# The last two tiles' search for 256 keys moves from the latent projections into the latent attention sweep, with its rows in the places of h

## The chip, the cores and the metric

The kernel runs on one core of a Trainium2 chip. The metric is the device time of one execution in microseconds. Five engines matter: TensorE (PE, with its weight loads PEld), VectorE (DVE), ScalarE (ACT), GpSimd (POOL) and SyncE (SP), which issues the DMA transfers here. Each engine runs its own instructions in order.

## The reference

Two layers. Each normalises x (2048 positions, 1024 wide), projects it, and mixes it in four groups of heads, whose gated outputs are joined and projected back.

```python
y_a = stick_breaking(a_q, a_k, a_v)                    # group A, 4 heads of 64
cq, ckv = rms_norm(b_cq, ...), rms_norm(b_ckv, ...)    # group B, latents of 256 and 128
qb, kv = cq @ mla_w_uq, ckv @ mla_w_ukv                # 4 heads, 64 + 32 rotary
y_b = softmax_attention(q, k, v_b, 96 ** -0.5)
# group C: an indexer scores all visible keys of a query and keeps the best 256
score = sum over 4 index heads of iw * relu(iq . ik / 8)
top_val, top_idx = lax.top_k(score, 256)
y_c = softmax over those keys only
# group D: two softmaxes a head, subtracted: w = p1 - lam * p2
y_d = rms_norm(diff_attention(...), ...) * (1 - lam_init)
y = concatenate(silu(gate) * y_group); x = x + y @ w_out
```

All attention is causal by chunks of 64 keys. The queries go in 16 blocks (tiles) of 128, so tile i sees 128 (i + 1) keys.

## The kernel before, in words

**Sweeps.** A layer goes through the 16 tiles seven times, in the order a, h, d0, d1, b, c, o: group A with the indexer's scores (a); the projections of group B's latents and of two gates (h); the two halves of group D (d0, d1); the attention of group B on its latents, the latent sweep (b); the sparse attention (c); the output (o). `drive` (L1391) hands out, with tile t's attention, the load of h for tile t + 4, `prep` of tile t + 2 and `proj` of tile t + 3, across the ends of sweeps too; the weights of a sweep are handed out four and five tiles before it. So b's projection of tile 7 is handed out with b's tile 4.

**Order.** The program is Python that writes instructions; a planner then orders them. It simulates the engines and gives each the earliest instruction, by the order of writing, whose data and buffers are there. `at` (L306) shifts a part's place in that order: the search is written in 30 places ahead, projections and preparations 10 places behind (`LATER`). On the chip the order of each engine is then fixed.

**Buffers.** The pool `wk` has tiles by name with a number of places: `g2` (4), `h_hi` and `h_lo` (2 each, 4096 bytes a partition each), `x4a`, `x4b`, `x4c` (1 each), `hl` (2). Two rings of bytes hold what changes size: `ring` (R1) the weights, keys and values of the sweeps, `rows` (R2) the rows of attention (`rw`), of scores (`sc`) and of the search (`sg`). A row of tile i has 512 (i + 1) bytes a partition: 7680 for tile 14, 8192 for tile 15.

**The search.** `ci_score` (L490) writes a tile's scores to DRAM. `ci_search` (L527) takes a pair of tiles, loads their rows (L535) and looks for a threshold that 256 keys exceed. ScalarE counts with a sign and an accumulator (L549); VectorE turns the count into the next threshold in some 18 small instructions (L551, L612 to L633). There are two counts at fixed points, then eight rounds. Then four long passes a tile on VectorE mark the keys (L641, L643, L644, L651), and the marks go to DRAM (L653), from where sweep c's `prep_c` (L983) takes them. Each `yield` ends a step. `SEARCH` says where a pair's search is written: pairs up to (10, 11) within sweep a, (12, 13) and (14, 15) both with tile 3 of h (`search_at`, called in `proj_h`). The rows of tiles 14 and 15 lie in `ring` (`INBIG`), the others in `rows`, where there is room for tile 13's only when earlier ones are done.

**The projections.** `proj_d` (L1026) copies v out of PSUM (L1033), takes squares on ScalarE, sums on VectorE (L1039), 1/sqrt on GpSimd (`rstd`, L282 and L283), the rotation on VectorE (L1092 to L1095), and GpSimd writes the parts `hl` (L197, L191) that TensorE then transposes. `proj_b` loads a tile's latents into a `g2` (L1241), splits them into two further `g2`, and uses `g2` for the squares (L1253 to L1256), for t, r, u and w too: nine a tile.

Of the kernel before, what the change touches and what calls it, by code (L numbers as in the profile page):

```python
# [10 lines left out]
F32 = mybir.dt.float32  # L11
# [4 lines left out]
AF = mybir.ActivationFunctionType  # L16
OP = mybir.AluOpType
AX = mybir.AxisListType
# [4 lines left out]
D = 1024  # L23
# [3 lines left out]
BIG = 1.0e30  # L27
# [9 lines left out]
EARLY = (10, 11, 9)  # L37
SEARCH = {("a", 4): ((2, 3),), ("a", 7): ((4, 5),), ("a", 10): ((6, 7),), ("a", 15): ((8, 9), (10, 11)), ("h", 3): ((12, 13), (14, 15))}
HL = 2
QA = 3  # L40
EV = (0.6, 1.0, 0.6)
INBIG = (14, 15)
ST = 2
# [12 lines left out]
LATER = {"search": -30, "prep": 10, "proj": 10, "first": 10, "second": 0}  # L56
R1 = 88832
R2 = 30592

# [48 lines left out]
class Trunk:  # L108
    def __init__(self, ctx, tc, I, out, layers=2):
        self.tc, self.nc, self.I, self.out, self.layers = tc, tc.nc, I, out, layers  # L110
        nc = self.nc
        e = ctx.enter_context
# [16 lines left out]
        ct = self.cst.tile  # L129
# [11 lines left out]
        nc.gpsimd.memset(self.nego, -1.0)  # L141
        self.eps = ct([128, 1], F32, name="eps")
        nc.vector.memset(self.eps, EPS)
# [4 lines left out]
        self.junk = ct([128, S], I8, name="junk")  # L148
        self.chkA = ct([128, layers], F32, name="chkA")
        self.chkC = ct([128, layers, NT], F32, name="chkC")  # L150
        nc.vector.memset(self.chkC, float(TOPK))
        self.ev = 0

    def constants(self):
# [371 lines left out]

    def ci_search(self, l, b):  # L527

        nc, wk = self.nc, self.wk
        yield 100.0  # L530
        tl, G = b, len(b)
        ns = [128 * (i + 1) for i in tl]
        Sg = [(self.ring if i in INBIG else self.rows).tile([128, n], F32, name="sg") for i, n in zip(tl, ns)]
        for g in range(G):
            nc.sync.dma_start(Sg[g], self.sc[tl[g]])  # L535
        stt = lambda nm: wk.tile([128, G], F32, name="st_" + nm, bufs=ST)
        V = nc.vector
        tt, ts, sst, cp = V.tensor_tensor, V.tensor_scalar, V.scalar_tensor_tensor, V.copy_predicated
# [7 lines left out]
        def count(dst, th):  # L546

            for g in range(G):
                nc.scalar.activation(self.junk[:, :ns[g]], Sg[g], AF.Sign, bias=th[:, g:g + 1], scale=-1.0,  # L549
                                     accum_out=dst[:, g:g + 1])  # L550
            sst(dst, dst, -0.5, nh, op0=OP.mult, op1=OP.add)  # L551
# [3 lines left out]
        for g in range(G):  # L555
            V.max(m8[:, g, :], Sg[g][:, ::32])
            V.tensor_reduce(a[:, g:g + 1], Sg[g][:, :ns[g] - 64:32], axis=AX.X, op=OP.max, apply_absolute_value=True)
        zt = stt("zt")
# [79 lines left out]
        for g in range(G):  # L638
            i = tl[g]
            ge = wk.tile([128, S], I8, name="ge", bufs=1)[:, :ns[g]]  # L640
            ts(ge, Sg[g], T[:, 0, g:g + 1], 0.0, op0=OP.is_ge, op1=OP.add, accum_out=T[:, 1, g:g + 1])  # L641
            yield 0.0
            sst(Sg[g], ge, -BIG, Sg[g], op0=OP.mult, op1=OP.add)  # L643
            V.max(ex[:, g, 1:9], Sg[g])  # L644
            ts(rc[:, g:g + 1], T[:, 1, g:g + 1], -1.0, float(TOPK), op0=OP.mult, op1=OP.add)
            oh = wk.tile([128, 9], F32, name="st_oh")
            ts(oh, self.iota9, rc[:, g:g + 1], None, op0=OP.is_equal)
            V.tensor_tensor_reduce(oh, oh, ex[:, g, :], 1.0, 0.0, OP.mult, OP.add, sp[:, g:g + 1])
            yield 0.0
            ck = self.chkC[:, l, i:i + 1]  # L650
            sst(ge, Sg[g], sp[:, g:g + 1], ge, op0=OP.is_lt, op1=OP.subtract, accum_out=ck)  # L651
            ts(ck, ck, -1.0, float(ns[g]), op0=OP.mult, op1=OP.add)
            nc.sync.dma_start(self.out_of[i][:, :ns[g]], ge)  # L653
            yield 0.0
# [23 lines left out]
    def search_at(self, l, sweep, i):  # L678
        if not self.short:
            return  # L680
        gs = [self.at(LATER["search"], self.ci_search(l, b)) for b in SEARCH.get((sweep, i), ())]
        while gs:
            for g in list(gs):
                if next(g, None) is None:
                    gs.remove(g)

    def prep_a(self, l, i, st):
# [549 lines left out]
    def proj_b(self, l, i, st):  # L1237
        nc, wk = self.nc, self.wk
        yield 1600.0
        raw = self.g2([128, 3, 128])  # L1240
        nc.sync.dma_start(raw, self.cT[i])  # L1241
# [9 lines left out]
                       kv[:, :, 64:])  # L1251
        sq = self.g2([128, 4, 96])
        nc.scalar.activation(sq[:, :, :64], qv[:, :, :64], AF.Square, scale=0.125)  # L1253
        nc.scalar.activation(sq[:, :, 64:], qv[:, :, 64:], AF.Square, scale=32 ** -0.5)
        sk = self.g2([128, 4, 64])
        nc.scalar.activation(sk, kv[:, :, :64], AF.Square, scale=0.125)  # L1256
# [5 lines left out]
        t = self.g2([128, 8, 64])  # L1262
        r = self.g2([128, 5, 32])
        nc.sync.dma_start(r[:, 4, :], self.kr[i])
# [7 lines left out]
        yield 0.0  # L1272
        u = self.g2([128, 5, 32])
        w = self.g2([128, 5, 32])
        cs = wk.tile([128, 2, 64], F32, name="ci_cs")[:, :, :32]
# [235 lines left out]
```

## Time and profile before

| | us |
|---|---|
| median of 3 runs | 4197.03 |
| lowest and highest | 4191.1, 4197.24 |
| profiled execution, its own time | 4202.9 |
| span of its instructions | 4201.0 |
| TensorE busy | 3887.7 |
| VectorE busy | 2784.5 |
| ScalarE busy | 2321.2 |
| GpSimd busy | 1361.0 |

Times in the rows below count from the start of the span. The mean granted clock of TensorE is 0.951, as a share of full speed. In the first layer the sweeps lie roughly so: a to 450, h to 620, d0 to 980, d1 to 1255, b to 1615, c to 1930, o to 2100; the second layer repeats this.

### The profile page before, as it was taken

The numbers are of one execution on the slowest core, as the hardware profiler recorded it, in microseconds if no ns is written. First come the engines' busy times: TensorE is split into PE (matmuls) and PEld (weight loads), VectorE is DVE, ScalarE is ACT, GpSimd is POOL, SyncE is SP. The second block draws the span as 40 slices with busy tenths as digits, with TensorE's granted clock in tenths as the row PEclk, the third lists the DMA queues.
The fourth block names the chain that finished last, engine by engine and source line by source line (L and its number), as shares of the span: only waits on it lengthen the run. The fifth ranks groups of instructions, "written<-read, shape, count | busy, mean of one in ns | idle before, by whom it ended". The sixth has DMA issues, their size and how long they took to land. (4 is left out here: it accounts for less than half of the span.)

```text
span 4201.0 us, 75220 instructions
## 1 busy us (share of the span) xinstructions
PE 3887.7 (93%) x25833; PEld 3279.2 (78%) x25833; DVE 2784.5 (66%) x10279; ACT 2321.2 (55%) x4799; POOL 1361.0 (32%) x2188
## 2 busy tenths in 40 slices
PE   7998998898978999999999989868989889999998
PEld 7887887777857888778888878767788668877787
DVE  3798677886876655663348975778768666556622
ACT  4566577565655555463246656675656555455621
POOL 2233222454553433310033331224445544232100
PEclk9999997899989999999999999879999799999999
DMA  4323562232210013225422246522222100132144
GB/s 135 104 97 122 176 192 88 76 93 78 86 38 23 18 38 106 77 67 175 166 98 98 94 127 204 161 66 79 87 86 82 36 23 18 39 111 72 59 142 141
DMA packets 227880, 396.49 MB, mean 94 GB/s; under 512 B 66336, under 2 KB 150432, under 8 KB 226976
## 3 DMA queue, kind: packets, MB, share of 16 engines
q1 hardware_dynamic: 227488, 391.59, 29.5%
q8 instruction: 207, 3.39, 0.3%
q14 instruction: 185, 1.52, 0.1%
HBM read 279.00 MB, written 112.49 MB: 93 GB/s over the span
## 5 line engine op out<-in xcount | busy, mean ns | idle before, releaser
L267 PE MATMUL pj<-w_hi,h_hi 128*128 128x384 f32 (+4 forms) x2560 | 875.8, 350 | 48.5 <-ACT w_hi L204 19.0
L268 PE MATMUL pj<-w_lo,h_hi 128*128 128x384 f32 (+4 forms) x2560 | 861.8, 344 | 8.4 <-POOL w_lo L191 6.3
L860 ACT ACTIVATE rw<-rw,at_mn 128x896 f32<-128x896 f32 (+15 forms) x512 | 616.1, 1205 | 191.4 <-DVE at_mn L859 161.0
L294 PE MATMUL tp<-ident,rw 128*128 128x128 f32 x3264 | 535.2, 288 | 55.4 <-DVE rw L1125 31.6
L267 PEld LDWEIGHTS pj<-w_hi,h_hi 128*128 128x128 f32 x2560 | 504.7, 197 | 81.1 <-ACT w_hi L204 21.3
L296 ACT COPY pt<-tp 128x512 f32<-128x512 f32 (+3 forms) x689 | 356.4, 530 | 381.5 <-PE tp L294 356.6
L268 PEld LDWEIGHTS pj<-w_lo,h_hi 128*128 128x128 f32 x2560 | 504.6, 197 | 34.8 <-POOL w_lo L191 9.9
L271 PE MATMUL pj<-w_hi,h_lo 128*128 128x384 f32 (+4 forms) x2560 | 527.5, 337 | 0.6 <-POOL h_lo L191 0.5
L294 PEld LDWEIGHTS tp<-ident,rw 128*128 128x128 f32 x3264 | 381.0, 145 | 167.0 <-issue 69.8
L271 PEld LDWEIGHTS pj<-w_hi,h_lo 128*128 128x128 f32 x2560 | 436.7, 191 | 24.7 <-issue 8.8
L856 DVE TENSOR_SCALAR_CACHE_REDUCE rw<-s 128x512 f32<-128x512 f32 x576 | 382.6, 683 | 92.8 <-PE s L850 76.2
L282 POOL TENSOR_SCALAR rs<-ss 128x2 f32<-128x2 f32 (+4 forms) x224 | 52.5, 234 | 1103.3 <-DVE ss L963 323.0
L549 ACT ACTIVATE junk<-sg,st_T 128x1152 int8<-128x1152 f32 (+4 forms) x224 | 293.7, 1311 | 68.1 <-DVE st_T L633 51.0
L283 POOL TENSOR_TENSOR rs<-rs,mhalf 128x8 f32<-128x8 f32 (+5 forms) x256 | 307.8, 1203 | 18.7
L850 PE MATMUL s<-dk,qa 96*128 96x512 f32 (+3 forms) x640 | 240.6, 426 | 40.0 <-DVE rw L856 21.1
L297 DVE COPY pt<-tp 128x512 f32<-128x512 f32 (+3 forms) x247 | 152.9, 619 | 158.7 <-PE tp L294 141.6
L850 PE MATMUL s<-bk,qa 128*128 128x512 f32 (+6 forms) x960 | 255.6, 394 | 2.6 <-DVE at_mn L854 2.0
L197 POOL TENSOR_SCALAR hl<-g 128x256 fp32r<-128x256 f32 (+1 forms) x384 | 148.8, 401 | 327.7 <-DVE g L463 104.4
L854 DVE CUSTOM_DVE_ANT_0 rw<-s,maskR 128x128 f32<-128x128 f32 (+3 forms) x400 | 187.2, 478 | 71.1 <-PE s L850 69.8
L294 PE MATMUL pj<-identr,hl 128*128 128x128 f32 (+1 forms) x1280 | 171.1, 256 | 58.3 <-POOL hl L191 32.0
L516 ACT ACTIVATE pt<-s 128x512 f32<-128x512 f32 (+3 forms) x304 | 158.0, 548 | 106.0 <-PE s L514 59.7
L191 POOL TENSOR_TENSOR hl<-g,hl 128x128 fp32r<-128x128 f32 (+1 forms) x384 | 215.9, 577 | 0.4
(271 smaller groups left out, 8249.5 us busy)
## 6 DMA issues: line engine op xcount, KB each, us to landing
h_hi<-hT SPq DMA_DIRECT2D x128, 512.0 KB, 3.8
h_lo<-hT SPq DMA_DIRECT2D x128, 512.0 KB, 5.0
x4a<-x SPq DMA_DIRECT2D x32, 512.0 KB, 4.5
hT<-h_hi SPq DMA_DIRECT2D x32, 512.0 KB, 2.6
hT<-h_lo SPq DMA_DIRECT2D x32, 512.0 KB, 3.4
x4a<-y SPq DMA_DIRECT2D x32, 512.0 KB, 3.6
x4b<-gate SPq DMA_DIRECT2D x32, 512.0 KB, 3.6
x4c<-x SPq DMA_DIRECT2D x32, 512.0 KB, 4.4
```

The source lines that it names most:

```text
L191: self.nc.gpsimd.tensor_sub(o, a, b)
L267: nc.tensor.matmul(p[:, :n], hi[:, k, :], whi[k], start=(k == 0), stop=False)
L268: nc.tensor.matmul(p[:, :n], hi[:, k, :], wlo[k], start=False, stop=False)
L271: nc.tensor.matmul(p[:, :n], lo[:, k, :], whi[k], start=False, stop=(k == kt - 1))
L283: nc.gpsimd.tensor_tensor(r, r, self.mhalf[:, :n], op=OP.pow)
L294: nc.tensor.transpose(p[:m, j, :].bitcast(dst.dtype), s.bitcast(dst.dtype), ident)
L296: return nc.scalar.copy(dst, p[:m, :len(srcs), :])
L549: nc.scalar.activation(self.junk[:, :ns[g]], Sg[g], AF.Sign, bias=th[:, g:g + 1], scale=-1.0, accum_out=dst[:, g:g + 1])
L850: nc.tensor.matmul(p[:, :w], x, y, start=(k == 0), stop=(k == len(ops) - 1))
L854: nc.vector.tensor_tensor_reduce(o, p[:, :w], b, -scale, 3.0e38, OP.add, OP.min, m)
L856: nc.vector.tensor_scalar(o, p[:, :w], -scale, None, op0=OP.mult, op1=OP.min, accum_out=m)
L860: nc.scalar.activation(rw, rw, AF.Exp, bias=mn, scale=-1.0, accum_out=ls)
```

## The change

The pair (14, 15) is taken out of `SEARCH` and `INBIG` goes. The pair's search is started with b's projection of tile 7, and each of b's projections from there on writes four steps of it (`search_along`), without the shift by 30 places. Its rows lie in the two places of h (`h_tiles`), which b doesn't use; since a place holds 1024 elements, each row is cut in two parts (1024 and 896, 1024 and 1024), and every count, pass and sum over a row is made of two. The sampled maximum works on a copy of the samples. In `proj_b` the squares go to `x4b`, and r, u and w to one tile `x4c`, in place of five `g2`. `ring` has 88,704 bytes for 88,832, `rows` 30,720 for 30,592; the small tiles eps and chkA become one.

```diff
-SEARCH = {..., ("h", 3): ((12, 13), (14, 15))}
+SEARCH = {..., ("h", 3): ((12, 13),)}
-INBIG = (14, 15)
+SPREAD = {7: (14, 15)}
+STEPS = 4
-R1 = 88832
-R2 = 30592
+R1 = 88704
+R2 = 30720
...
-        self.eps = ct([128, 1], F32, name="eps")
+        small = ct([128, 1 + layers], F32, name="small")
+        self.eps = small[:, 0:1]
-        self.chkA = ct([128, layers], F32, name="chkA")
+        self.chkA = small[:, 1:1 + layers]
...
-    def ci_search(self, l, b):
+    def ci_search(self, l, b, h_free=False):
-        Sg = [(self.ring if i in INBIG else self.rows).tile([128, n], F32, name="sg") for i, n in zip(tl, ns)]
+        C = 1 if h_free is False else 2
+        if C == 1:
+            Sg = [[self.rows.tile([128, n], F32, name="sg")] for n in ns]
+        else:
+            Sg = []
+            for n in ns:
+                x, y = [t.bitcast(F32).rearrange("p a b -> p (a b)") for t in self.h_tiles()]
+                Sg.append([x, y[:, :n - D]])
         for g in range(G):
-            nc.sync.dma_start(Sg[g], self.sc[tl[g]])
+            for k, x in enumerate(Sg[g]):
+                nc.sync.dma_start(x, self.sc[tl[g]] if C == 1 else self.sc[tl[g]][:, k * D:k * D + x.shape[1]])
...
         def count(dst, th):
+            cn = [dst] if C == 1 else [stt("cn"), stt("cm")]
             for g in range(G):
-                nc.scalar.activation(self.junk[:, :ns[g]], Sg[g], AF.Sign, bias=th[:, g:g + 1], scale=-1.0,
-                                     accum_out=dst[:, g:g + 1])
+                for x, d in zip(Sg[g], cn):
+                    nc.scalar.activation(self.junk[:, :x.shape[1]], x, AF.Sign, bias=th[:, g:g + 1], scale=-1.0,
+                                         accum_out=d[:, g:g + 1])
+            if C == 2:
+                tt(dst, cn[0], cn[1], op=OP.add)
...
+    def search_along(self, l, i):
+        if not self.short:
+            return
+        if i in SPREAD:
+            self.along = self.ci_search(l, SPREAD[i], True)
+        for _ in range(STEPS):
+            if self.along is None or next(self.along, None) is None:
+                self.along = None
+                return
...
     def proj_b(self, l, i, st):
         yield 1600.0
+        self.search_along(l, i)
...
-        sq = self.g2([128, 4, 96])
+        squares = self.x4("b", [128, 640])
+        sq = squares[:, :384].rearrange("p (h c) -> p h c", h=4)
-        sk = self.g2([128, 4, 64])
+        sk = squares[:, 384:].rearrange("p (h c) -> p h c", h=4)
-        r = self.g2([128, 5, 32])
+        turned = self.x4("c", [128, 3, 5, 32])
+        r = turned[:, 0]
-        u = self.g2([128, 5, 32])
-        w = self.g2([128, 5, 32])
+        u, w = turned[:, 1], turned[:, 2]
```

The long passes and the maxima of the last step are cut in the same way, with an addition or a second maximum over the two results.

## Rows read from the trace of the kernel before

**Rows 1.** The page: TensorE over the span; hl writes (busy us, mean ns).

```profile
PE 3887.7 (93%) x25833; PEld 3279.2 (78%) x25833; DVE 2784.5 (66%) x10279; ACT 2321.2 (55%) x4799; POOL 1361.0 (32%) x2188
...
L197 POOL TENSOR_SCALAR hl<-g 128x256 fp32r<-128x256 f32 (+1 forms) x384 | 148.8, 401 | 327.7 <-DVE g L463 104.4
```

**Rows 2.** Stretches: length, busy us by engine, PEclk, DMA share, GB/s.

```profile
620.00:780.00 160.00, 120.75 (x638) 105.07 (x638) 130.58 (x683) 110.22 (x212) 53.04 (x94) 0.77 0.29 86
990.00:1150.00 160.00, 158.07 (x1246) 142.25 (x1247) 125.16 (x461) 102.79 (x244) 82.15 (x149) 1.00 0.32 97
1160.00:1340.00 180.00, 148.01 (x996) 114.34 (x993) 117.99 (x400) 99.18 (x227) 84.70 (x138) 0.84 0.11 30
1340.00:1500.00 160.00, 156.06 (x1294) 128.40 (x1292) 110.13 (x395) 93.77 (x184) 70.63 (x130) 1.00 0.07 19
2200.00:2450.00 250.00, 238.13 (x1476) 206.76 (x1474) 224.98 (x882) 161.29 (x354) 86.45 (x119) 0.98 0.29 100
2690.00:2870.00 180.00, 127.15 (x654) 111.42 (x652) 143.33 (x718) 120.58 (x221) 54.49 (x92) 0.73 0.29 88
```

**Rows 3.** Lines L535, L653 (min/median/max ns, first and last start us).

```profile
L535 SPq DMA_DIRECT2D sg<-sc x7: 319/422/471, 460.5 to 597.3; - x7
...
L535 SPq DMA_DIRECT2D sg<-sc x7: 320/382/886, 2527.4 to 2692.8; - x7
...
L653 SPq DMA_DIRECT2D out_of<-ge x4: 319/323/551, 721.7 to 767.2; - x4
...
L653 SPq DMA_DIRECT2D out_of<-ge x4: 319/324/552, 2805.8 to 2858.4; - x4
```

**Rows 4.** Line L1033, v of tiles 3 to 10: d0, d1, both layers.

```profile
L1033 ACT COPY dv<-pj x8: 244/266/266, 667.5 to 805.1; 128x128 f32<-128x128 f32 x8
...
L1033 ACT COPY dv<-pj x8: 266/266/267, 1000.0 to 1087.6; 128x128 f32<-128x128 f32 x8
...
L1033 ACT COPY dv<-pj x8: 245/266/268, 2747.7 to 2898.1; 128x128 f32<-128x128 f32 x8
...
L1033 ACT COPY dv<-pj x8: 266/266/267, 3095.9 to 3183.5; 128x128 f32<-128x128 f32 x8
```

**Rows 5.** Waits of 700 to 780: us in total, times, longest.

```profile
PEld pj L294 <- POOL hl L191: 14.0, 3, 9.3
...
POOL rs L282 <- DVE st_md L627: 12.5, 1, 12.5
```

**Rows 6.** Groups by form, ScalarE, line L549 (busy us, mean ns).

```profile
L549 ACT ACTIVATE junk<-sg,st_T 128x2048 int8<-128x2048 f32 x16 | 32.1, 2006 | 0.1
...
L549 ACT ACTIVATE junk<-sg,st_T 128x1920 int8<-128x1920 f32 x16 | 30.4, 1898 | 2.3 <-DVE st_md L627 1.5 <-DVE st_up L612 0.3 <-DVE st_T L604 0.2
...
L549 ACT ACTIVATE junk<-sg,st_T 128x1024 int8<-128x1024 f32 x16 | 18.4, 1151 | 0.1
...
L549 ACT ACTIVATE junk<-sg,st_T 128x896 int8<-128x896 f32 x16 | 16.7, 1043 | 19.4 <-DVE st_T L633 16.8 <-DVE st_T L604 2.6
```

**Rows 7.** Timeline of VectorE, 696.5 to 699.2, first and last row.

```profile
696.62 0.16 DVE L551 SCALAR_TENSOR_TENSOR st_T<-st_T,st_nh 128x2 f32<-128x2 f32 x1 [2.21 <-ACT junk L549]
...
698.98 0.16 DVE L633 COPY_PREDICATED st_T<-st_nd,st_sp 128x2 f32<-128x2 int32 x1
```

**Rows 8.** Groups by form, VectorE, 620 to 780.

```profile
L641 DVE TENSOR_SCALAR_CACHE_REDUCE ge<-sg,st_T 128x2048 int8<-128x2048 f32 x1 | 2.3, 2347 | 0.3 <-DMA out_of<-ge 0.3
...
L641 DVE TENSOR_SCALAR_CACHE_REDUCE ge<-sg,st_T 128x1664 int8<-128x1664 f32 x1 | 1.9, 1945 | 0.0
```

**Rows 9.** Line L247, loads of h, 1130 to 1170.

```profile
L247 SPq DMA_DIRECT2D h_hi<-hT x2: 319/350/382, 1140.3 to 1158.8; - x2
```

**Rows 10.** Timeline of all engines, 741.5 to 744.2.

```profile
741.53 2.02 DVE L643 SCALAR_TENSOR_TENSOR sg<-ge,sg 128x1792 f32<-128x1792 int8 x1
741.78 2.41 POOL L197 TENSOR_SCALAR hl<-g 128x256 fp32r<-128x256 f32 x2 [1.47 <-DVE g L1043]
```

**Rows 11.** Line L1241, loads of a tile's latents, 1270 to 1345.

```profile
L1241 SPq DMA_DIRECT2D g<-cT x4: 319/319/320, 1276.0 to 1330.5; - x4
```

More of the change, by code (lines that the diff above doesn't have):

```diff
@@ L37 @@
 EARLY = (10, 11, 9)
-SEARCH = {("a", 4): ((2, 3),), ("a", 7): ((4, 5),), ("a", 10): ((6, 7),), ("a", 15): ((8, 9), (10, 11)), ("h", 3): ((12, 13), (14, 15))}
+SEARCH = {("a", 4): ((2, 3),), ("a", 7): ((4, 5),), ("a", 10): ((6, 7),), ("a", 15): ((8, 9), (10, 11)), ("h", 3): ((12, 13),)}
 HL = 2
@@ L555, in ci_search @@
         for g in range(G):
-            V.max(m8[:, g, :], Sg[g][:, ::32])
-            V.tensor_reduce(a[:, g:g + 1], Sg[g][:, :ns[g] - 64:32], axis=AX.X, op=OP.max, apply_absolute_value=True)
+            if C == 1:
+                V.max(m8[:, g, :], Sg[g][0][:, ::32])
+                V.tensor_reduce(a[:, g:g + 1], Sg[g][0][:, :ns[g] - 64:32], axis=AX.X, op=OP.max, apply_absolute_value=True)
+            else:
+                sm = self.g2([128, 64])
+                w = ns[g] // 32
+                V.memset(sm, -BIG)
+                V.tensor_copy(sm[:, :32], Sg[g][0][:, ::32])
+                V.tensor_copy(sm[:, 32:w], Sg[g][1][:, ::32])
+                V.max(m8[:, g, :], sm)
+                V.tensor_reduce(a[:, g:g + 1], sm[:, :w - 2], axis=AX.X, op=OP.max, apply_absolute_value=True)
         zt = stt("zt")
@@ L640, in ci_search @@
             ge = wk.tile([128, S], I8, name="ge", bufs=1)[:, :ns[g]]
-            ts(ge, Sg[g], T[:, 0, g:g + 1], 0.0, op0=OP.is_ge, op1=OP.add, accum_out=T[:, 1, g:g + 1])
-            yield 0.0
-            sst(Sg[g], ge, -BIG, Sg[g], op0=OP.mult, op1=OP.add)
-            V.max(ex[:, g, 1:9], Sg[g])
+            parts = [(ge if C == 1 else ge[:, k * D:k * D + x.shape[1]], x) for k, x in enumerate(Sg[g])]
+            ac = [T[:, 1, g:g + 1]] if C == 1 else [stt("cn")[:, 0:1], stt("cm")[:, 0:1]]
+            for (e, x), d in zip(parts, ac):
+                ts(e, x, T[:, 0, g:g + 1], 0.0, op0=OP.is_ge, op1=OP.add, accum_out=d)
+            if C == 2:
+                tt(T[:, 1, g:g + 1], ac[0], ac[1], op=OP.add)
+            yield 0.0
+            for e, x in parts:
+                sst(x, e, -BIG, x, op0=OP.mult, op1=OP.add)
+            if C == 1:
+                V.max(ex[:, g, 1:9], Sg[g][0])
+            else:
+                e2 = self.g2([128, 2, 8])
+                for k, x in enumerate(Sg[g]):
+                    V.max(e2[:, k, :], x)
+                V.max(ex[:, g, 1:9], e2.rearrange("p a b -> p (a b)"))
             ts(rc[:, g:g + 1], T[:, 1, g:g + 1], -1.0, float(TOPK), op0=OP.mult, op1=OP.add)
@@ L650, in ci_search @@
             ck = self.chkC[:, l, i:i + 1]
-            sst(ge, Sg[g], sp[:, g:g + 1], ge, op0=OP.is_lt, op1=OP.subtract, accum_out=ck)
+            ac = [ck] if C == 1 else [stt("cn")[:, 0:1], stt("cm")[:, 0:1]]
+            for (e, x), d in zip(parts, ac):
+                sst(e, x, sp[:, g:g + 1], e, op0=OP.is_lt, op1=OP.subtract, accum_out=d)
+            if C == 2:
+                tt(ck, ac[0], ac[1], op=OP.add)
             ts(ck, ck, -1.0, float(ns[g]), op0=OP.mult, op1=OP.add)
@@ L685, in search_at @@
                     gs.remove(g)
+    def search_along(self, l, i):
[5 more added lines that the diff above has]
+            if self.along is None or next(self.along, None) is None:
+                self.along = None
+                return
     def prep_a(self, l, i, st):
```

## The prediction

> **What bounds the kernel now.** I read the page first: TensorE is busy 93% of a span of 4201.0 us [rows 1], so the question is where it isn't, or runs at half clock. The stretches answer that [rows 2]. In the first layer's d1, 990 to 1150, TensorE is busy 158.1 of 160 us at a granted clock of 1.00, although VectorE is busy 78% and ScalarE 64% of it. In d0's head, 620 to 780, it is busy only 120.8 of 160 us, at 0.77: much of it ran at 1.2 GHz and not at 2.4. Counted at full clock that is 120.8 x 0.77 = 93 us, 67 less than the stretch is long. The second layer's d0 head, 2690 to 2870, has 127.2 x 0.73 = 93 of 180 us: 87 less. The head of the latent sweep (b), 1160 to 1340, is the other poor stretch, 148.0 x 0.84 = 124 of 180; its later part, 1340 to 1500, is full (156.1 of 160 at 1.00).
>
> What stands in d0's head is the search. The rows of tile 13 are loaded at 597.3 and 2692.8, and the last results of the pairs (12, 13) and (14, 15) leave at 767.2 and 2858.4 [rows 3]: the poor stretches. d0 and d1 do the same work on two halves of the heads, so their pace can be compared. The copies of v after eight successive projections (tiles 3 to 10) take 667.5 to 805.1 in d0 and 1000.0 to 1087.6 in d1: 137.6 against 87.6 us, 50.0 more. In the second layer 150.4 against 87.6, 62.8 more [rows 4]. Together 112.8 us. The waits of 700 to 780 give the mechanism: GpSimd stands 12.5 us behind an instruction of the search (st_md) on VectorE before it can make an rstd, and TensorE's weight loads wait 14.0 us for the hl that GpSimd makes from that [rows 5]. VectorE and ScalarE work in order, and the projection's chain goes through both.
>
> **What leaves d0's head.** Each search counts ten times: two end points, eight rounds. A round of (14, 15) is 1.898 + 2.006 = 3.90 us of ScalarE [rows 6], ten are 39 us. On VectorE a round's chain takes 696.62 to 699.14, 2.5 us [rows 7], so eight are 20; the four long passes over 1920 and 2048 elements go by 2.347 us for 2048 and 1.945 for 1664 [rows 8], which is 1.047 ns an element and 0.20 us fixed: 4 x 3968 x 1.047 ns + 8 x 0.20 = 18.2 us; with about 4 for the start it is some 43. Taking this from 620 to 780 leaves VectorE (130.6 - 43)/160 = 55% and ScalarE (110.2 - 39)/160 = 45%, well under what d1 carries with TensorE full.
>
> What does that return? The pair (12, 13) stays, and can't start before its rows are free, as now. By share of work (14, 15 are 3968 of 7424 elements, 53%) the excess falls by 60 us; if all of it goes, by 113. The pair left needs its own ten counts and passes, about half of the 170 us that both took. After that d0 runs at d1's pace, 87.6/7 = 12.5 us a tile. If nothing is gained up to then and the pair ends near 703 (first layer) and 2795 (second), five tiles at 12.5 remain before the tenth's copy, or four: 703 + 62 = 765 against 805.1, and 2795 + 50 = 2845 against 2898.1. That is 40 + 53 = **-93 us**, between the bounds, and I take it.
>
> **What the latent sweep gets.** The count is cut in two instructions a tile, 1024 and 896 or 1024 elements: 3 x 1.151 + 1.043 = 4.50 us a round [rows 6], 45 us a layer. VectorE gets an addition in each round (2.7 x 8 = 21), passes with twice the fixed part (16.6 + 16 x 0.20 = 19.8) and some 5 for start and sampled maximum: 46 us a layer. The steps are given out from tile 7's projection on, but the planner moves work forward when its data and room are there: c's first two h loads, for projections that come after b's, stand at 1140.3 and 1158.8 [rows 9]. They take h's two places, and the search, handed out earlier, will take these ahead of them. So it should begin near 1160, in the poor head. From 1160 to 1500 VectorE would have 118.0 + 110.1 + 46 = 274 of 340 us (81%), ScalarE 99.2 + 93.8 + 45 = 238 (70%): d1's level. The nearest row with a search beside dense work is 2200 to 2450: VectorE 90%, TensorE 238.1 x 0.98 = 233 of 250, 6.7% lost [rows 2]. 6.7% of 160 us is 11 a layer: **+22 us**. Bounds: nothing, if it fits the gaps; 45 + 46 = 91 a layer, +182, if chain after chain lies open.
>
> One thing is not free. The pair of hl writes on GpSimd at 741.78 took 2.41 us, where such a write takes 0.40 on average, and ended when a two-input pass of the search on VectorE (2.02 us from 741.53) ended [rows 1, 10]. The Trainium skill, GPSIMD Engine Reference, section 1 (Specifications), says that GpSimd shares its SBUF interfaces with VectorE and contends with instructions of two SBUF inputs; by that rule eight half passes a layer of some 1.2 us would hold up b's projection chain, up to 20 us more in all. The trace agrees that it happens. I add nothing, because the passes do it in d0 already; it lies within the bound.
>
> **The rest.** Projection b no longer takes its squares and turned parts from the four g2 places but from x4b and x4c, idle there. Now four loads of a tile's latents are issued from 1276.0 to 1330.5, 18.2 us apart [rows 11]: one tile after another, each load waiting for a g2 that the tile before still holds. With four g2 a tile and not nine, the load and the split run ahead. Other links stay (rstd, hl's two places), and x4b and x4c are single, so the squares and turned parts of a tile wait for those before. The head lacks 56 us of full-clock TensorE; I take 10 a layer, **-20 us**, between 0 and -50. c's bias, which uses x4b and x4c, must then wait for b's last projection; it has until c's tile 2.
>
> The rows' ring now holds four rows of tile 14 (4 x 7680 bytes), before three; a fourth row saves at most the wait for one pass over 1920 elements, about 1.9 us, in eight sweeps: 0 to -15, I take 0. The weights' ring is freed of 15,872 bytes, so d0's weights may come sooner; the deficits of the heads (67 + 87) exceed the 113 by 41 us, the bound for this. I take 0. On SP's queue two row loads and two stores move from h to b and the loads become four; none stands before a load that TensorE waits for, unless the search runs so late that c's h loads stand behind it, with b's latents and y stores queued after them. eps and chkA in one tile cost nothing: no one waits on them.
>
> **The sum.** 4202.9 (the profiled execution; 1.9 outside the span) - 93 + 22 - 20 = 4111.9. That execution is 5.9 above the median of the runs, 4197.0, so by the median **4106 us**.
>
> **Rivals.**
> - The payment eats it (slower). Round and count alternate, VectorE waits for ScalarE's count, and in b the exp and the copies out of PSUM, which TensorE waits for, are in the same two queues. In full it is +182: 4197 - 93 + 182 = 4286. It decides from the point where over half (93 of 182) lies open. Against it: TensorE keeps 0.99 in d1 with the same loads.
> - The clock. Short waits in b let the granted clock fall, as in d0's head (0.77). Were it so from 1340 to 1500, 156 us of TensorE would take 203: +47 a layer, which cancels the 93: 4197. Against it: 2200 to 2450, with VectorE at 90%, kept 0.98. The Trainium skill, TensorE: Matmul & The Clock Gate, section "A second HAM failure mode: psum-queue depth-cycling", says that short recurring idle of TensorE makes its clock swing and costs time between bursts; by that rule a full TensorE is no safety. The trace shows such swings in the heads only.
> - The remaining pair keeps d0's head poor: its rounds go on with the same interruptions, and only the work share returns: -60 + 22 = 4159. For it: the pair keeps its high priority.
> - More than I take: all 113 return, the search hides, b's head opens by 50: 4034. For it: the remaining load of both heads.
>
> **Chances.** Forecast 0.52 (its own range 4065 to 4140), remaining pair 0.19, more 0.12, clock 0.08, payment 0.09. Changes below 0.2% (8 us) can't be told from none. Faster takes the first three and a little of the clock's, 0.84; same 0.06; slower 0.10. The range leaves out the payment, some of the clock's and the far part of "more": 4040 to 4185.
>
> **What would show it.** v's copies of tiles 3 to 10 in d0 under 105 us in both layers, at a clock above 0.85 in 620 to 780; the last result of (12, 13) before 710; counts of 1024 and 896 elements from 1160 to about 1450, TensorE still above 150 of 160 us in b's second part; b's latents under 18 us apart. It is wrong if the pair that stays still ends after 740, if b's later part falls below 1.00, or if c's h loads wait for the search.

## The result, and the profile after

The changed kernel takes 4230.3 us (median of 6 runs, 4219.7 to 4231.8), the kernel before 4196.0 (6 runs): a ratio of 1.0073, 95% interval 1.0063 to 1.0083. By the ratio it is slower by some 31 us (the medians are 34 apart), where 91 us less were forecast. The profiled execution is 4229.6 us, its span 4227.8.

TensorE's busy time in the span is 3898 us against 3888, so most of the 27 us by which the span grew is time in which it idles. Four stretches of the kernel after, with the columns of [rows 2]: length, busy us of PE, PEld, DVE, ACT and POOL, granted clock, DMA share, GB/s.

```profile
620.00:780.00 160.00, 136.22 (x905) 123.61 (x906) 112.04 (x515) 93.55 (x219) 65.91 (x123) 0.88 0.33 99
1160.00:1340.00 180.00, 147.93 (x1038) 116.31 (x1037) 119.52 (x470) 106.79 (x246) 88.56 (x150) 0.88 0.09 25
1340.00:1500.00 160.00, 137.62 (x1066) 109.90 (x1065) 119.67 (x496) 98.92 (x192) 51.82 (x90) 0.95 0.10 31
1500.00:1650.00 150.00, 142.17 (x1077) 116.78 (x1075) 76.13 (x241) 70.30 (x142) 44.77 (x80) 0.94 0.24 73
```

d0's head is better: 136.2 us of TensorE at 0.88, against 120.8 at 0.77. The loser is b's later part, 1340 to 1500, which was full (156.1 at 1.00): 137.6 at 0.95. The copies of v after tiles 3 to 10 in d0, in both layers, and the last two marks stored in h's search, answer to [rows 3, 4]:

```profile
L1086 ACT COPY dv<-pj x8: 244/266/283, 664.5 to 768.8; 128x128 f32<-128x128 f32 x8
...
L695 SPq DMA_DIRECT2D out_of<-ge x2: 320/436/551, 702.1 to 714.5; - x2
...
L1086 ACT COPY dv<-pj x8: 266/267/284, 2754.6 to 2859.5; 128x128 f32<-128x128 f32 x8
```

137.6 us became 104.3, and 150.4 became 104.9. The stores of outputs (y) show how far that carries. Before, these are d1's last four outputs, then all of b's and c's in the first layer; after, d1's last three, then b's and c's:

```profile
L1150 SPq DMA_DIRECT2D y<-o x4: 319/319/393, 1178.4 to 1255.0; - x4
...
L902 SPq DMA_DIRECT2D y<-o x32: 319/320/550, 1260.9 to 1931.7; - x32
...
L1203 SPq DMA_DIRECT2D y<-o x3: 319/335/551, 1164.5 to 1219.7; - x3
...
L955 SPq DMA_DIRECT2D y<-o x32: 319/320/384, 1225.3 to 1949.9; - x32
```

The last output of d1 is stored at 1220, before at 1255. By the end of c that lead is gone: from d1's last output to c's last it was 677 us and is 730 in the first layer, 679 and 739 in the second.

Where it went can be read from SyncE's queue. This is its timeline, loads of latents (g<-cT), c's loads of h and the search's stores alone; columns: start, duration, engine, line, operation, out and in.

```profile
1344.80 0.38 SPq L1295 DMA_DIRECT2D g<-cT  x1
1360.40 0.38 SPq L1295 DMA_DIRECT2D g<-cT  x1
1438.19 0.32 SPq L250 DMA_DIRECT2D h_hi<-hT  x1
1439.26 0.32 SPq L695 DMA_DIRECT2D out_of<-ge  x1
1439.63 0.42 SPq L250 DMA_DIRECT2D h_lo<-hT  x1
1440.11 0.48 SPq L1295 DMA_DIRECT2D g<-cT  x1
1455.22 0.43 SPq L1295 DMA_DIRECT2D g<-cT  x1
```

From tile 2's to tile 11's at 1360 the loads of latents come 13 to 24 us apart, and then none comes for 80 us (91 in the second layer, 3462 to 3553). Tile 12's stands behind c's first load of h and the store of tile 14's marks, and both wait for the search's end. GpSimd, which splits the latents, shows it among the waits of 1390 to 1460:

```profile
POOL g L200 <- DMA g<-cT: 37.9, 1, 37.9
```

Why the search ends so late is in its own lines. First the counts (ScalarE) between 1090 and 1320, then the maximum over the sampled copy, in both layers:

```profile
L563 ACT ACTIVATE junk<-h_hi,st_zt x4: 1150/1150/1166, 1106.3 to 1139.6; 128x1024 int8<-128x1024 f32 x4
...
L563 ACT ACTIVATE junk<-h_hi,st_T x3: 1150/1151/1163, 1299.2 to 1317.5; 128x1024 int8<-128x1024 f32 x3
...
L582 DVE MAX8 st_m<-g x4: 205/210/215, 1295.3 to 3397.3; 128x8 f32<-128x64 f32 x4
```

The rows came early and the two end points were counted by 1146, even before the poor head. Then nothing, for 150 us: the maximum over the sample, from which the rounds start, runs at 1295.3. The poor head was not used.

### The profile page after: what moved, and what is told of

Read it like the earlier page. It is cut to its first block, busy times and chain, and to the rows that moved or that the text cites. A ratio compares the mean times of both kernels' runs of the same rounds, so it can differ in the third digit from the quotient of the medians.

```text
span 4227.8 us, 75305 instructions
## 1 busy us (share of the span) xinstructions
PE 3898.1 (92%) x25833; PEld 3267.4 (77%) x25833; DVE 2784.2 (66%) x10347; ACT 2328.3 (55%) x4879; POOL 1348.6 (32%) x2188
## 5 line engine op out<-in xcount | busy, mean ns | idle before, releaser
L270 PE MATMUL pj<-w_hi,h_hi 128*128 128x384 f32 (+4 forms) x2560 | 865.6, 346 | 41.5 <-ACT w_hi L207 18.7
L271 PE MATMUL pj<-w_lo,h_hi 128*128 128x384 f32 (+4 forms) x2560 | 852.1, 341 | 4.4 <-POOL w_lo L194 2.9
L270 PEld LDWEIGHTS pj<-w_hi,h_hi 128*128 128x128 f32 x2560 | 495.3, 194 | 75.9 <-ACT w_hi L207 21.2
L271 PEld LDWEIGHTS pj<-w_lo,h_hi 128*128 128x128 f32 x2560 | 495.4, 194 | 28.0 <-issue 5.2
L563 ACT ACTIVATE junk<-sg,st_T 128x1152 int8<-128x1152 f32 (+4 forms) x192 | 231.3, 1205 | 77.8 <-DVE st_T L659 62.0
L297 PEld LDWEIGHTS pj<-identr,hl 128*128 128x128 f32 (+1 forms) x1280 | 138.7, 143 | 109.6 <-POOL hl L200 39.8
```

Source lines behind the costliest of these rows:

```text
L270: nc.tensor.matmul(p[:, :n], hi[:, k, :], whi[k], start=(k == 0), stop=False)
L271: nc.tensor.matmul(p[:, :n], hi[:, k, :], wlo[k], start=False, stop=False)
L297: nc.tensor.transpose(p[:m, j, :].bitcast(dst.dtype), s.bitcast(dst.dtype), ident)
L563: nc.scalar.activation(self.junk[:, :x.shape[1]], x, AF.Sign, bias=th[:, g:g + 1], scale=-1.0, accum_out=d[:, g:g + 1])
```

## The experiments

Five theories. **One**: the places of g2 are handed out in the order in which tiles are written, and the search has two small ones there: the sampled copy (sm) must wait until the projections written before it have given up theirs, and the load of latents written after the search's last small tile (e2) must wait for that. **Two**: the search's own work in b costs. **Three**: c's first loads of h come too late. **Four**: the new places of the squares and turned parts cost. **Five**: two rows no longer pass through the weights' ring, so that all later tiles lie elsewhere in it. All ratios are to the kernel before, run beside; 0.0010 is 4.2 us.

| run | what differs | us | ratio (95%) |
|---|---|---|---|
| own_e2 | after, e2 in its own place | 4183.8 | 0.9966 (0.9953 to 0.9978) |
| own_sm | after, sm in its own place | 4195.1 | 0.9999 (0.9987 to 1.0011) |
| own_both | after, both | 4209.1 | 1.0033 (1.0021 to 1.0046) |
| nosearch | after, no search of 14, 15 | 4143.6 | 0.9879 (0.9862 to 0.9895) |
| ring_nosearch | nosearch, ring moved on | 4112.4 | 0.9798 (0.9782 to 0.9814) |
| ring_after | after, ring moved on | 4223.8 | 1.0069 (1.0052 to 1.0086) |
| ring_e2 | own_e2, ring moved on | 4176.0 | 0.9958 (0.9943 to 0.9972) |
| ring_sm | own_sm, ring moved on | 4187.6 | 0.9967 (0.9953 to 0.9981) |
| before_nosearch | before, no search of 14, 15 | 4138.0 | 0.9856 (0.9835 to 0.9878) |
| before_rows | before, new ring sizes | 4178.4 | 0.9950 (0.9932 to 0.9968) |
| before_x4 | before, new places in b | 4209.6 | 1.0033 (1.0020 to 1.0045) |
| half | ring_e2, half the rounds | 14696.8 | 3.5001 (3.4943 to 3.5060) |
| half_quiet | the same, guard fixed | 4174.9 | 0.9952 (0.9936 to 0.9967) |
| ring_e2_g2 | ring_e2, b's squares in g2 | 4169.4 | 0.9936 (0.9920 to 0.9953) |
| ring_both_g2 | the same, sm in its own place | 4178.2 | 0.9958 (0.9944 to 0.9972) |
| sp9_g2 | ring_e2_g2, from tile 9 | 4157.4 | 0.9918 (0.9901 to 0.9934) |
| gate7 | ring_e2_g2, first counts held back | 4159.8 | 0.9910 (0.9894 to 0.9927) |
| gate9 | sp9_g2, first counts held back | 4164.4 | 0.9926 (0.9910 to 0.9943) |

**The two small tiles.** own_e2 has the second of these edits, own_sm the first, own_both both; the places taken are idle then.

```diff
-                sm = self.g2([128, 64])
+                sm = wk.tile([128, 64], F32, name="ge", bufs=1)
...
-                e2 = self.g2([128, 2, 8])
+                e2 = wk.tile([128, 2, 8], F32, name="st_m8", bufs=1)
```

own_e2:

> The changed kernel, with one edit: the small tile that gathers the two halves' maxima at the end of the search (e2) has a place of its own and no longer takes its turn in the four places of g2. Theory 1 (the turn in g2 ties the latent projections to the search: tile 12's load of latents can only be issued after the search's last pass): the hole of 80 us between the loads of tiles 11 and 12 goes, the sweep b keeps its 18 us a tile, and 40 to 80 us in all come back: 4150 to 4190. Theory 2 (the search's own work on ScalarE and VectorE is what costs): the hole only moves, 4215 to 4235. Theory 3 (c's first loads of h stand behind the search, and c starts late): those loads still come near 1440, so at most 15 us come back, 4215 to 4230.

own_sm:

> The changed kernel, with one edit: the sampled copy at the start of the search (sm) has a place of its own, the small tile at its end (e2) still takes a g2. Theory 1: the search no longer stops between 1146 and 1295; its rounds begin near 1160 in the poor head of b, its end and c's first loads of h come 60 to 130 us sooner, the hole before tile 12 shrinks or goes: 4130 to 4190. Theory 2: the same work in the same queues, 4215 to 4235. Theory 3: c's first h loads come sooner, 4150 to 4200, and it can't be told from theory 1 by this run alone.

own_both:

> The changed kernel with places of their own for both small tiles of the search, the rest as it is. Theory 1: search from about 1150, no hole, near the forecast: 4110 to 4170. It would be worse than that if the stores of the search's marks and c's first h loads, which are now ahead of tile 8's latents in SyncE's queue, end up waiting for a search that is still running when tile 8 is due: then a hole of the same kind stands at tile 8, 4170 to 4230. Theory 2: 4215 to 4235 either way, since the work is the same. Theory 3: 4150 to 4200.

One tile of 64 bytes a partition was worth 45 us (1.0073 to 0.9966). SyncE's queue in own_e2:

```profile
1362.75 0.38 SPq L1295 DMA_DIRECT2D g<-cT  x1
1400.59 0.48 SPq L1295 DMA_DIRECT2D g<-cT  x1
1410.43 0.42 SPq L1295 DMA_DIRECT2D g<-cT  x1
1451.66 0.32 SPq L250 DMA_DIRECT2D h_hi<-hT  x1
1452.03 0.42 SPq L1295 DMA_DIRECT2D g<-cT  x1
1452.73 0.32 SPq L695 DMA_DIRECT2D out_of<-ge  x1
```

Two loads now come before the search's end, and TensorE has 151.1 of 160 us at 0.98 in 1340 to 1500, not 137.6 at 0.95. c's first load of h, however, comes later than before this edit (1451.7, not 1438.2), so theory three is not where the time was. In own_sm the sampled maximum runs at 1107.5, and the rounds' counts from 1156 to 1281, as theory one says; b's head pays for it (146.0 of 180 us at 0.83, after 147.9 at 0.88), and 31 us come back (4195, where theory one gave 4130 to 4190). The second tie is still there: the rounds are over at 1290, but the first maximum that is written to e2 runs at 1399.7, and between the loads of tiles 11 and 12 there are still 46 us (1365 to 1411). The counts of the rounds, and that maximum in VectorE's timeline:

```profile
L563 ACT ACTIVATE junk<-h_hi,st_T x16: 1141/1152/1172, 1156.0 to 1277.5; 128x1024 int8<-128x1024 f32 x16
```

```profile
1399.70 1.22 DVE L681 MAX8 g<-h_hi 128x8 f32<-128x1024 f32 x1
```

own_both gives less than either. At tile 8, where a hole was feared, the load comes 28 us after tile 7's (1304 and 1332), so the hole is small. The profiled run is 20 us longer than own_e2's, and 15 of these lie before d1's last output (7 and 9 in the two layers), where the rounds now begin; that an early start costs there is likely, not shown, and why own_both is slower than own_sm too stays open.

**What the search costs.** nosearch puts a constant in the place of the search:

```diff
-            self.along = self.ci_search(l, SPREAD[i], True)
+            for t in SPREAD[i]:
+                ge = self.wk.tile([128, S], I8, name="ge", bufs=1)[:, :128 * (t + 1)]
+                self.nc.vector.memset(ge, 0)
+                self.nc.sync.dma_start(self.out_of[t][:, :128 * (t + 1)], ge)
```

> The changed kernel without the search of tiles 14 and 15: their marks are stored as zeros from tile 7's projection on, nothing else is taken out. It gives what the change returns before any payment: theories 1 to 3 all expect the forecast without its payment, 4202.9 - 93 - 20 = 4090 (4070 to 4110). If it is above 4150, d0 did not return what it seems to have, or b got slower by its new places for squares and turned parts (theory 4).

It misses what all the theories said by 53 us. So the search costs 81 us (1.0073 less 0.9879), and even without it the change falls far short of its forecast. The profiled runs of after and nosearch say where the search is paid: after is 16 us longer on the way from a's last output to d1's (10 and 6 in the two layers), 65 in b (25 and 40), 4 in c. own_e2 gives back 42 of the 65 in b and almost nothing elsewhere. Against the kernel before, nosearch has b a little shorter (354 and 350 us, before 359 and 355), but c longer: 349 and 348 us from b's last output to c's, before 318 and 324. In c's head GpSimd and the copies of k show the cause. A line of the waits of 1490 to 1640, the copies of k between 1490 and 1600 (count, ns, first and last start), and the stretch:

```profile
POOL w_hi L200 <- PE y L990: 32.1, 1, 32.1
```

```profile
L299 ACT CAST ck<-pj x4: 372/377/390, 1555.7 to 1590.3; 128x256 fp32r<-128x256 f32 x4
```

```profile
1500.00:1650.00 150.00, 136.51 (x958) 109.56 (x957) 70.56 (x244) 65.23 (x138) 41.83 (x73) 0.94 0.26 81
```

GpSimd waits 32 us to write a part of the output's weights, and c's first k is copied at 1555.7, 59 us after its v (before: 11): both only when b's last product of v (y, L990) is done. Both lie in the weights' ring. The changed kernel has the same wait, 25.8 us long (after, 1490 to 1640):

```profile
POOL w_hi L200 <- PE y L987: 25.8, 1, 25.8
```

**The ring.** In sweep h two tiles of the old rows' sizes are taken from it again:

```diff
+        if (sweep, i) == ("h", 3):
+            gs.append(self.fill(14, 15))
...
+    def fill(self, *tl):
+        yield 100.0
+        for i in tl:
+            t = self.ring.tile([128, 128 * (i + 1)], F32, name="sg")
+            self.nc.sync.dma_start(t[:, :128], self.sc[i][:, :128])
+        yield 0.0
```

ring_nosearch:

> The kernel without the search of tiles 14 and 15 (marks stored as zeros), and with the weights' ring moved on in sweep h as in the kernel before: two tiles of 7680 and 8192 bytes are taken from it there, and only their first 128 columns are loaded. Theory 5: since the two rows no longer pass through the weights' ring, what comes later lies at other places of it, and in c's head k of the sweep c and the output's weights wait for b's last product of v (GpSimd: 32.1 us, one wait), which makes c some 25 us longer a layer. Then this kernel regains 30 to 60 us against the one without the search at 4143.6: 4083 to 4113, which is also the forecast without its payment (4090). Theory 4 (the new places of the squares and turned parts make c longer): no change, 4138 to 4148.

ring_after:

> The changed kernel with the weights' ring moved on in sweep h as before, by two tiles of the same size, of which 128 columns are loaded. Theory 5: 25 us a layer come back in c's head: 4170 to 4205, at or under the kernel before. Theory 4: 4225 to 4235.

ring_e2:

> The changed kernel with both remedies: the tile at the search's end (e2) has its own place, and the ring is moved on as before. If theories 1 and 5 are two separate losses, their gains add: 4183.8 less 30 to 60 is 4124 to 4154, faster than the kernel before by 1.0 to 1.7%. If they are one and the same wait seen twice, it stays at 4175 to 4190.

ring_sm:

> The changed kernel with the ring moved on as before and the sampled copy (sm) in a place of its own; the small tile at the end (e2) in g2. The search then runs from about 1170 to 1290 in the poor head of b, and b was as long as without a search when this was tried without the ring (355 against 354 us in the first layer, 366 against 350 in the second). Theory 1 with theory 5: 4195.1 less 10 to 30: 4165 to 4185. If c's head pays again what the ring returns, as in ring_after: 4185 to 4195.

Without the search the shift was worth 34 us (0.9879 to 0.9798). c's first k comes at 1514.7, 11 us after its v, GpSimd waits 1.0 us and not 32 for a product of v, and the stretch is nearly full at a granted clock of 1.00:

```profile
L299 ACT CAST ck<-pj x5: 370/373/382, 1514.7 to 1591.9; 128x256 fp32r<-128x256 f32 x5
```

```profile
1500.00:1650.00 150.00, 146.16 (x1074) 120.24 (x1074) 83.11 (x285) 73.20 (x160) 50.65 (x86) 1.00 0.29 96
```

With the search the gain doesn't arrive: 2 us in ring_after and 3 in ring_e2, both inside their intervals, 13 in ring_sm. In ring_after c is 28 and 18 us shorter in the two layers (323 in the first, not 351), but b is 18 and 7 longer (397 in the first, not 379), and the way to d1's last output 3 and 11. Theory five is right in its mechanism: c gets its time back. Why b and the sweeps before it lose it again where there is a search is not shown.

**The parts alone.** before_nosearch takes the pair (14, 15) out of sweep h, stores zeros for its marks and keeps the ring's two tiles. before_rows has R1 = 88704, R2 = 30720 and the merged small tile. before_x4 has proj_b's new places:

```diff
-        sq = self.g2([128, 4, 96])
+        squares = self.x4("b", [128, 640])
+        sq = squares[:, :384].rearrange("p (h c) -> p h c", h=4)
...
-        r = self.g2([128, 5, 32])
+        turned = self.x4("c", [128, 3, 5, 32])
+        r = turned[:, 0]
```

before_nosearch:

> The kernel before without the search of tiles 14 and 15 (their marks are stored as zeros in sweep h; the weights' ring is taken as before, 128 columns of each row are loaded). Nothing of the rest of the change is in it, so it measures the term d0 alone. The forecast's term is -93: 4195.9 - 93 = 4103; the segments of the traces so far (d0 and d1 together 46 and 48 us shorter) give 4102. Rival: only the share of work returns, -60: 4136. With 4112.4 of the same kernel with the change's other parts (ring_nosearch), the difference of the two is what those parts cost where there is no search: +14 as by before_x4, so 4098, or 0, so 4112.

before_rows:

> The kernel before with one part of the change alone: the rows' ring has 30,720 bytes and the weights' ring 88,704, with eps and the first check in one small tile. The forecast gave it 0 (to -15): 4181 to 4196. If it explains why the pair's removal returns 84 us with the change's other parts and 61 without, it is 15 to 30 us faster: 4166 to 4181. If the shorter weights' ring costs, it is above 4200.

before_x4:

> The kernel before with one part of the change alone: the latent projection's squares and turned parts lie in x4b and x4c and not in the four places of g2. The forecast gave this part -20 us, 4177 (0 to -50). Between 4190 and 4200 it would be worth nothing: the head of b is then not held by g2. Above 4205 (theory 4) the new places cost c its early bias and are a part of the loss.

Taking the pair out of h returns 60 us: from a's last output to d1's it is 28 and 35 us shorter in the two layers. v's copies of tiles 3 to 10 take 104.1 us there (670.5 to 774.6), and 116.4 in the second layer. The new ring sizes, forecast at nothing, return 21, and in the profiled run all of it before d1's last output (5 and 16 us); which of the two rings does it, this run doesn't separate. The new places, forecast at -20, cost 14; the profiled run of that kernel is the fastest of its six (4200.5), so its trace can't show where, and that c pays, as theory four had it, is not shown. Summed, the three are -67; the kernel that has all three and no search, ring_nosearch, stands at -85. The intervals of the four make the difference uncertain by some 15 us, so the 18 us between are little more than that; they stay open.

**Rounds or ends.** half has `NITER // 2` rounds in this search, half_quiet also `V.memset(ck, float(TOPK))` for its guard.

> The kernel with both remedies (ring_e2, 4176.0; ratio to before 0.9958), with four rounds and not eight in the search of tiles 14 and 15, and the count that guards their result replaced by its wanted value, so that the second, long path isn't taken (their marks may be off). The search costs 64 us there. Theory 2 (paid by the round): four of eight rounds fewer return some 25 us, 4145 to 4160 (0.988 to 0.992 of before). Paid at the two ends: 4168 to 4178.

half told nothing of this: with four rounds its guard's count isn't met, and the kernel ran its second, long path (56,825 matmuls, not 25,833). half_quiet tells it. With four rounds of eight gone in both layers, the time is that of ring_e2 (0.9952 against 0.9958, 2.5 us less, where 25 were expected; each ratio is good to some 6 us). The stretch 1340 to 1500 in ring_e2, and then in half_quiet:

```profile
1340.00:1500.00 160.00, 149.99 (x1195) 121.50 (x1196) 128.26 (x527) 108.00 (x207) 58.97 (x108) 0.98 0.08 24
```

```profile
1340.00:1500.00 160.00, 149.95 (x1170) 121.65 (x1171) 120.65 (x440) 91.04 (x175) 58.93 (x109) 0.96 0.11 32
```

ScalarE has 17 us less to do there and VectorE 8, and TensorE is busy for the same time, at 0.96 and not 0.98. Theory two is wrong where it counts by the round. But it isn't how late the search ends either. Its two marks are stored 78 and 81 us sooner in half_quiet than in ring_e2 (in this order: ring_e2, half_quiet), and c's first load of h is issued at 1399 and not at 1477:

```profile
L695 SPq DMA_DIRECT2D out_of<-ge x2: 319/352/384, 1478.1 to 1506.8; - x2
...
L698 SPq DMA_DIRECT2D out_of<-ge x2: 319/320/320, 1400.4 to 1425.5; - x2
```

In the second layer they come 73 and 74 us sooner. Nothing comes back for it. What is left as the place of the 64 us is the search's start in d1's tail, the rounds that remain and the long passes; the profiled runs of ring_e2 and ring_nosearch put 23 us of them before d1's last output and 25 in b, and what of these parts costs it stays open. half, the run on the long path, was expected so:

> The kernel with both remedies (ring_e2, 4176.0), with four rounds and not eight in the search of tiles 14 and 15 (their marks may then be off). The search still costs 4176.0 - 4112.4 = 64 us there. If that is paid by the round (theory 2: ten counts and eight chains of VectorE), four rounds fewer return about 0.4 of it, 25 us: 4145 to 4160. If it is paid at the search's two ends (loads and first counts in d1's tail, sampled copy in g2, stores, c's first loads of h), nothing or little returns: 4168 to 4178.

**The order.** In ring_e2_g2 proj_b's tiles are back in g2; ring_both_g2 also has sm's own place. sp9_g2 has `SPREAD = {9: (14, 15)}` and `STEPS = 5`. The gated ones make the first end points wait for the sample:

```diff
-        V.memset(zt, 0.5 * TINY)
+            ts(zt, a, 0.0, 0.5 * TINY, op0=OP.mult, op1=OP.add)
...
-            V.memset(zt2[:, g:g + 1], -(ns[g] + 0.5) * TINY)
+                ts(zt2[:, g:g + 1], a[:, g:g + 1], 0.0, -(ns[g] + 0.5) * TINY, op0=OP.mult, op1=OP.add)
```

ring_e2_g2:

> The kernel with both remedies (ring_e2), and the latent projection's squares and turned parts back in g2 as in the kernel before. If the new places cost 14 us, as by before_x4, this is 4176 - 14 = 4162 (4155 to 4170), the best so far. If the search's sampled copy, which still takes a g2, is then held up longer by nine g2 a tile and not four, the search starts later still and ends at the end of b: 4180 to 4220.

ring_both_g2:

> The kernel with both remedies and the squares back in g2 (ring_e2_g2, 4169.4; ratio 0.9936), and now the search's first small tile (sm) in its own place too, so that the rounds run in b's head. The stores and c's first loads of h stand in SyncE's queue around tile 8's latents. If the search is over by then (1300 to 1310), it runs in the poor head at TensorE's spare time: 4140 to 4165. If not, a hole stands at tile 8 as in own_both: 4170 to 4200.

sp9_g2:

> The kernel ring_e2_g2 (4169.4) with the search's steps given out from tile 9's projection on, five with each tile, and not from tile 7's, four with each. Its first counts then stay out of d1's tail only if the planner does not move them forward all the same; its end, and with it c's first loads of h, comes after b's last latents. If d1's tail was what the search still cost (10 to 14 us a layer): 4145 to 4160. If c's head now waits for h: 4175 to 4200.

gate7:

> The kernel ring_e2_g2 (4169.4, 0.9936 of before) with its first two end points made from the sampled maximum (times zero, plus the same constant), so that the counts at them wait for the sampled copy and leave d1's tail. If the early counts are what makes d1 end 10 to 14 us later a layer: d1's end near 1214, 4140 to 4155. If they are hidden there and what costs is the end of the search, which comes some 20 us later: 4170 to 4190.

gate9:

> The same edit in the kernel that starts the search at tile 9 (sp9_g2, 4157.4, 0.9918 of before). If the early counts cost: 4130 to 4145. If the end costs: the search, begun near 1345, would end near 1530, after c's first projections could have started, and c's head waits for its loads of h: 4165 to 4190.

Putting proj_b's tiles back in g2 returns 9 us (0.9958 to 0.9936), with intervals that overlap; sm's own place takes them again (ring_both_g2). The best versions, sp9_g2 and gate7, can't be told apart; they beat the kernel before by 0.8 and 0.9% and the changed one by 1.5 and 1.6%. sp9_g2 came out in the range that was given for a shorter tail of d1, but by luck: its first counts still run at 1110, the way to d1's last output is 2 and 3 us longer than in ring_e2_g2, and b is what got shorter (362 and 356 us, not 370 and 371). The gate moves the first counts from 1110 to 1295, as its lines show (the counts; a row of SyncE's timeline), and d1's last output in the first layer from 1225 to 1217.

```profile
L563 ACT ACTIVATE junk<-h_hi,st_zt x4: 1149/1156/1168, 1295.2 to 1306.0; 128x1024 int8<-128x1024 f32 x4
```

```profile
1217.12 0.39 SPq L1218 DMA_DIRECT2D y<-o  x1
```

That is 11 us in all, with intervals that overlap, and in the second layer the way to d1's last output gained nothing (774 against 771 us), so it is likely, not shown. In gate9 the search ends at 1541, c is 10 and 12 us longer than in sp9_g2, and nothing is won.

## Why the prediction was wrong, by its own steps

The forecast was -91 us, and +31 was measured. Of the 122 us between, the search in b is 59, the relief of b's head and the weights' ring 34 each, what leaves d0's head 33; the rows' ring takes 21 off, and 18 more come off where the parts stand together.

- **What leaves d0's head, -93.** The mechanism was right, the size was not: 60 alone (51 to 69). The step that failed is the one from 703 and 2795 on, "After that d0 runs at d1's pace": in the changed kernel the pair that stays has its last mark stored at 714.5 and 2807.5, and v's copies take 104.3 and 104.9 us (104.1 and 116.4 in before_nosearch), not the 97.5 and 97.3 of the working (667.5 to 765, 2747.7 to 2845). The share of work gave 60, the bound that was passed over. That was the rival of the remaining pair, right in this term alone; that it hits 60 to the microsecond is partly luck, since v's copies fell by 67.5 us in before_nosearch (33.5 and 34.0), and some of that was lost again by d1's end.
- **The search in b, +22.** It was 81. The bounds (0 to 182) held it, the value didn't. What failed was the step "so it should begin near 1160, in the poor head", and "handed out earlier" was the error: its rows did come early, at 1103, but its sampled copy takes a place of g2 in its turn, and could not be read before 1295. The second such tile held tile 12's latents back, 80 us behind tile 11's where 13 to 24 are usual. 45 of the 81 us are shown to hang on that one (own_e2). How loaded VectorE and ScalarE are, on which the 22 was built, doesn't explain the rest: with half the rounds the time is the same (half_quiet). The sum of loads answered a question that wasn't the one that decided.
- **SyncE's queue, nothing "unless the search runs so late".** The condition came true: c's first h loads stood at 1438, with tile 12's latents behind them. It was written down as an exception and given no price. What this wait costs by itself no run shows; in half_quiet that load is issued 78 us sooner than in ring_e2, and the time is the same.
- **Relief of b's head, -20.** It was +14 alone. The step that failed is "each load waiting for a g2": [rows 11] show when the loads were issued, 18.2 us apart, and not what set that pace. With four g2 a tile and not nine, the head of b is no fuller (before_x4, 1160 to 1340: 146.1 us at 0.84, before 148.0 at 0.84), b takes 356 and 361 us (before 359 and 355), and in the changed kernel nine steps of the loads, 1193 to 1360, are still 18.6 us on average.
- **The rows' ring, 0 (to -15).** With the weights' ring 128 bytes shorter it returned 21 (13 to 28): a term put at nothing that was more than its bound, though the interval holds the 15.
- **The weights' ring, 0 (to -41).** The sign was wrong. Only the space given back was considered, not that every later tile is moved: 34 us, where no search hides it.
- **The rivals.** "The payment eats it" came nearest in effect, by a mechanism that it didn't have: 81 us lay open, close to its point of decision (over 93 of 182 if all else had held), with chains that were not the ones named. The clock was a minor part: in 1340 to 1500 the granted clock fell to 0.95, which is worth 7 of the 137.6 busy us, while 18.4 us of busy time are missing. The Trainium skill, TensorE: Matmul & The Clock Gate, section "A second HAM failure mode: psum-queue depth-cycling", has idle come back as a lower clock. The trace agrees in that the clock fell with the hole (0.95, and 0.98 in own_e2, where the hole is split into gaps of 38 and 42 us), but puts the larger part of the loss on idle time and not on the clock. GpSimd's port, for which up to 20 us were named, cost next to nothing in b: of the sixteen half passes with two inputs in the changed kernel (L675 and L691), two have GpSimd at work beside them, and one write, in GpSimd's timeline, took longer than usual there, 1.85 us where the median of its kind is 1.00:

```profile
1445.68 1.85 POOL L194 TENSOR_TENSOR g<-g,g 128x384 fp32r<-128x384 f32 x1
```

- **What was to show it.** Clock in 620 to 780 above 0.85: yes (0.88). v's copies under 105: just (104.3, 104.9). Last mark before 710: no. Counts from 1160: no. TensorE over 150 of 160 in b's second part, and its clock at 1.00: no. Latents under 18 us apart: no (18.6). c's h loads waiting for the search: yes, the sign of being wrong.

The measured pieces are -60 - 21 + 14 for the three parts, -18 that they gain together, +34 for the ring and +81 for the search: +30, and +31 was measured. The sum has to close, since the last three are differences between kernels on the way from before to after; it checks nothing. The order in which the ring and the search are counted is a choice; with the ring kept, the search takes 114 (1.0069 less 0.9798), and the ring then 2. Of the search's price, 36 us (own_e2 less nosearch) are not the second tie, and four of the eight rounds have no part in them that could be measured; the first counts are perhaps 11, the rest is open.

## What to carry to other kernels

Places handed out in rotation are a queue like any engine's: when a step is moved between others, list each place that it takes from a shared pool, who had it last and who gets it next. A tile taken out of a ring moves all that follow, so look up who holds the places that the next sweep's first tiles will get. Ask of a moved step where it can begin and what it holds up before pricing its work: here half of the rounds cost nothing that could be measured, and one tile of 64 bytes a partition cost 45 us.

## What was not expected of the hardware

Nothing of the chip by itself. What surprised was how much room two engines at 75% and 83% still leave: in sp9_g2, 1340 to 1500, with ScalarE at 120.4 and VectorE at 132.3 of 160 us, TensorE had 154.0 at a granted clock of 1.00. And the load of the two did not decide: with ScalarE at 108.0 and VectorE at 128.3, and with 91.0 and 120.7, TensorE had 150.0 both times (ring_e2 and half_quiet).
